# A two-layer attention encoder: the latent heads' keys and queries read from their banks at full height and put in place by transfers, weight sums two groups later

## The chip, the cores and the metric

One core of a Trainium2 chip runs the whole program in one launch. The metric is the device time of an execution in microseconds (us).

## What is computed

Two encoder layers on x of 1024 tokens by 1024 features, in float32; cut to what matters here:

```python
for layer in range(2):
    shift, scale, gate = split(silu(c) @ ada_w[layer] + ada_b[layer], 3)
    h = rms_norm(x, norm_w[layer]) * (1 + scale) + shift
    y = even_mixer(h) if layer == 0 else odd_mixer(h)
    x = x + gate * y
return rms_norm(x, final_norm)

# even_mixer: group A, dense grouped-query attention (8 heads, 2 of keys), and group B, latent attention:
cq, ckv = rms_norm(cq, g1), rms_norm(ckv, g2)      # 256 and 128 wide
qb = (cq @ w_uq).reshape(b, s, 8, 64 + 32)         # per head: 64 plain and 32 rotary
q_nope, q_rope = qb[..., :64], apply_rope(qb[..., 64:])
scores = (q_nope @ w_uk) @ ckv + q_rope @ k_rope   # 8 heads, one rotary key for all
out = concat([oa * silu(ga), ob * silu(gb)]) @ w_out
# odd_mixer: attention in a window of 128 either way, 16 heads, then (oc * silu(gc)) @ w_out
```

## The kernel before

Every matrix product takes its operands as a high and a low part, and three matmuls (high by high, low by high, high by low) make one product. The instructions are not issued in the order of the code. A recorder (L115 to L570) notes each operation, and `run` (L259) puts them into an order by a list schedule: each operation has a cost (`cost`, L224), a priority from its place, and a tile or PSUM bank to wait for (49 tiles of 128x1024 "u", 8 banks); a transfer's landing is guessed there too. `emit` (L543) issues the result, so every instruction of the profile carries L551. Within an engine the order is fixed from then on; SyncE's queue (SP) is such an engine, so a transfer that has to wait holds those behind it.

Layer 0's attention is 32 groups n = 0 to 31, each one head and one half of the queries: scores, maximum, exponential (tiles Pa in group A, Pb in group B), scaling by the reciprocal sum (POOL), transposes (TensorE), a copy and a difference that make the high and low part (hla, hlb), and the product with the values. n = 0 to 15 are group A, n = 16 to 31 group B, two groups to a head and four to a pair of heads. In a tile's name Pb201 is head 2, half 0, query block 1.

`before(n)` (L1467) hangs preparation on the groups:

- `b_heads(p, half)` (L1397) makes the keys and queries of heads 2p and 2p+1 for one half, at n = 15 (pair 0, both halves), 19 (pair 1), 22 and 23 (pair 2), 27 (pair 3); they are used from n = 16, 20, 24 and 28. A bank kn or qn of 128x512 holds two heads, 64 rows each. The tiles k1, k2, q1, q2 need the high and low part of a head on particular 64 rows, in part crossed over: q1 and k1 carry the high part on rows 0 to 63 and rotary rows above; k2 and q2 hold high and low parts one above the other. Every part is made by an operation of its own, 64 rows high: per call 6 copies on ACT, 4 differences on DVE, 2 copies on POOL.
- The rotary rows of the queries (qrh, qrl: high and low part, by ACT and DVE) go to memory as qr_sp by SP, and come back into q1[64:128] by four transfers of 128 KB a pair on POOL's queue.
- `weight_sums` (L1458), at n = 17 to 24 by the table `WS_AT`, makes the sums of blocks of the output weights for later: a load of 512 KB into a tile ws (SP), then up to three times an accumulating transfer from w_out (POOL's queue, `accum_op`) and a store of the sum so far (SP). Each link waits for the landing of the last; each tile of ws stays taken till its last store.

```python
1463        for a, b, k in [(3, 1, 0)] if third else [(1, 1, 1), (2, 0, 0), (4, 0, 1)]:
1464            nc.gpsimd.dma_start(out=t, in_=w(b, k), accum_op=ALU.add)
1465            nc.sync.dma_start(out=ws_sp[l, a, j], in_=t)
```

`wino_out` (L1569) is the output projection of each layer, in a form with fewer products that uses these sums. `layer1_after` (L1515) follows the second one: the statistic of the final norm for each half (`rstd_rows`, L742), and `finish`, which scales and stores. The last `finish` takes 256 tokens, of which the rows sit in four tiles xr110 to xr113. Layer 1's windowed attention writes its outputs by 64x128 blocks (`win_PV`, L1887) into tiles og1, multiplies them by the gates (`g_ft`, `g_ft_late`), and spills those that have to wait for the projection. At the start, TensorE does `WARM` transposes that nothing reads, 20 of them between the first statistic and the first product of layer 0.

Of the kernel before, what the change touches and what calls it, by code (L numbers as in the profile page):

```python
# [14 lines left out]
ALU = mybir.AluOpType  # L15
# [4 lines left out]
P = 128  # L20
# [34 lines left out]
WARM = (32, 14, 20)  # L55
# [4 lines left out]
WS_AT = {17: ((0, 0, False),), 18: ((0, 0, True),), 19: ((0, 1, False),), 20: ((0, 1, True),),  # L60
         21: ((1, 0, False),), 22: ((1, 0, True),), 23: ((1, 1, False),), 24: ((1, 1, True),)}
# [53 lines left out]
class Recorder:  # L115
# [143 lines left out]
    def run(self):  # L259
# [131 lines left out]
        while started < N or ev:  # L391

            for e in engs:
# [5 lines left out]
                while h:  # L399
# [12 lines left out]
                    if e == "SP" or (o.call[0].__name__ == "dma_start"):  # L412
                        nb = 4 * max(self._region(v)[2] * max(1, self._region(v)[3])
                                     for v in list(o.call[1]) + list(o.call[2].values())
                                     if isinstance(v, VP) or hasattr(v, "tensor"))
                        dma_free = max(dma_free, t + 1300) + nb / (205.0 if "accum_op" in o.call[2] else 410.0)
                        fin = dma_free + 500
                        busy[e] = t + (450 if e == "SP" else o.dur)
                    else:
                        fin = o.end  # L420
                        busy[e] = o.end
# [152 lines left out]
def encoder_kernel(ctx: ExitStack, tc: tile.TileContext, xt, ada_t, w_c1, w_c2, w_c3, w_g0, w_uq, w_ukv, w_out0, w_v1,  # L574
# [74 lines left out]

    def rstd_of(ss, n, width):  # L650
        v = SM("v")
        nc.gpsimd.tensor_scalar(v[:, :width], ss, 1.0 / n, EPS, op0=ALU.mult, op1=ALU.add)
        r = SM("r")
        nc.gpsimd.tensor_tensor(out=r[:, :width], in0=v[:, :width], in1=mhalf[:, :width], op=ALU.pow)
        return r
# [86 lines left out]
    def rstd_rows(accs, name):  # L742
# [21 lines left out]
        pr = PA(f"rb{name}")  # L764
        for j in range(nt):
            m_ = nc.tensor.transpose(out=pr[:, j * P:(j + 1) * P], in_=r[:, j:j + 1].broadcast_to([P, P]), identity=ident)
        if name == "x0" and WARM[2]:
            warm(WARM[2], m_)
        return pr[:, 0:n]
# [149 lines left out]
    for kc in range(KC):  # L919
# [3 lines left out]
        if kc == 0:  # L923
            rb0 = rows_copy(rp0, "x0")
# [3 lines left out]
        modulate(0, kc, chunk(xT[0], kc), None, hT0[0][kc], "normed")  # L928
        for i in range(E1):
            c1_part(i, w1[kc:], [kc])  # L930
# [466 lines left out]
    def b_heads(p, half):  # L1397
        e, o = 2 * p, 2 * p + 1
        for h in (e, o) if half == 0 else ():
            q1[h], q2[h], k2[h] = UR(f"q1{h}"), UR(f"q2{h}"), UR(f"k2{h}")  # L1400
            nc.gpsimd.dma_start(out=q1[h][64:96, :], in_=qr_sp[0][h * 32:(h + 1) * 32, :])
            nc.gpsimd.dma_start(out=q1[h][96:128, :], in_=qr_sp[1][h * 32:(h + 1) * 32, :])
# [6 lines left out]
        nc.scalar.copy(k1[0][0:64, c], ps[0:64, :])  # L1409
        nc.scalar.copy(k2[o][64:128, c], ps[64:128, :])  # L1410
        nc.scalar.copy(k1[1][0:64, c], ps[64:128, :])
        K2E(k2[e][0:64, c], f(k1[0][0:64, c]))
        sub(k2[e][64:128, c], ps[0:64, :], f(k1[0][0:64, c]))
        sub(k2[o][0:64, c], ps[64:128, :], f(k2[o][64:128, c]))
# [5 lines left out]
        nc.scalar.copy(q1[e][0:64, c], ps[0:64, :])  # L1420
        nc.scalar.copy(q1[o][0:64, c], ps[64:128, :])
        nc.scalar.copy(q2[e][64:128, c], ps[0:64, :])
        K2E(q2[o][0:64, c], f(q1[o][0:64, c]))
        sub(q2[e][0:64, c], ps[0:64, :], f(q1[e][0:64, c]))
        sub(q2[o][64:128, c], ps[64:128, :], f(q1[o][0:64, c]))
# [89 lines left out]
    def layer1_after():  # L1515
# [4 lines left out]
        def finish(res, half, c0, n, pr, last):  # L1520
            if not last:
                rb = rows_copy(pr, f"z{half}{c0}")

            with rec.at(shift=0 if last or half == 0 else 300):
                for k2 in (0, 1, 2, 3) if half == 0 else (2, 3, 0, 1):
# [4 lines left out]
                    if last or half == 1 and k2 > 1:  # L1530
                        r_ = pr if last else rb
                        (nc.vector if last else nc.gpsimd).tensor_tensor(
# [8 lines left out]
        def after(half, ft, c0, n, pos, res, last):  # L1541
# [17 lines left out]
            if pos == 7:  # L1559
                finish(res, half, c0, n, rstd_rows(sums, f"z{half}{c0}"), last)  # L1560
# [8 lines left out]
    def wino_out(l, w, kept, at, res_src, after):  # L1569
# [5 lines left out]
        def raw_o(half, k2, mark):  # L1575
            gone = [e for e in range(2) if 2 * k2 + e not in kept]
# [241 lines left out]
    def g_ft(p):  # L1818
        def evac(half, ps):
            sl = og1[p][:, half * 512:(half + 1) * 512]  # L1820
# [4 lines left out]
            if half == 1 and p < 6:  # L1825
                spill_out(1, p, og1.pop(p))
# [4 lines left out]
    def g_ft_late(p):  # L1831
        def evac(half, ps):
            if half == 0:
                g1[p] = U(f"g1{p}")
            sl = g1[p][:, half * 512:(half + 1) * 512]
            nc.scalar.activation(sl, ps, AF.Tanh, scale=0.5)
            nc.vector.scalar_tensor_tensor(out=sl, in0=sl, scalar=1.0, in1=ps, op0=ALU.add, op1=ALU.mult)
# [49 lines left out]
    def win_PV(g, i, Ps, lo, n, og):  # L1887
# [16 lines left out]
        for j in range(4):  # L1904
            r = slice((j % 2) * 64, (j % 2) * 64 + 64)
            nc.vector.tensor_tensor(out=og[j // 2][r, i * P:(i + 1) * P], in0=acc[0:64, j * P:(j + 1) * P],
                                    in1=tmp[:, j * P:(j + 1) * P], op=ALU.add)
# [32 lines left out]
    for g in range(4):  # L1940
        win_bias(g)
        for j in range(2):
            og1[2 * g + j] = U(f"og1{g}{j}")
        for i in range(NT):
# [3 lines left out]
            if True:  # L1948
                cur = (g, i) + win_S(g, i) + ([og1[2 * g], og1[2 * g + 1]],)
# [9 lines left out]
    for j in (6, 7):  # L1959
        nc.gpsimd.tensor_tensor(out=og1[j], in0=og1[j], in1=g1[j], op=ALU.mult)  # L1960
        keep[j] = og1[j]
# [81 lines left out]
```

## Time and profile before

| | us |
|---|---|
| median of three runs | 1184.37 (1184.14 to 1184.73) |
| the profiled execution | 1186.49 |
| its span, first to last instruction | 1184.7 |
| TensorE busy in the span | 1144.0 (97%) |
| VectorE / ScalarE / GpSimd busy | 961.6 (81%) / 699.6 (59%) / 608.0 (51%) |
| mean granted TensorE clock | 0.991 |

The span is 1.8 us short of the execution's time. A matmul row counts as busy from its start to its modelled end, so neighbouring rows overlap; what TensorE lost is read from the time in which it had nothing (rows 2 of the section below) and from stretches in which the granted clock is under 1.00.

### The profile page before, as it was taken

To read this page: it belongs to the slowest core of one execution; us is meant where nothing else is said; L and a number is where in the kernel's file an instruction comes from. 1 tells how busy PE (TensorE), PEld (TensorE's weight loads), DVE (VectorE), ACT (ScalarE), POOL (GpSimd) and SP (SyncE) were. 2 spreads that over 40 slices of the span, in tenths; PEclk is the share of its full clock that TensorE was granted. 3 is DMA by queue.
4 is the path that set the end of the run, shared out by engine and by line. 5 is a ranking of instruction groups with operands and counts; after the bars stand their busy time and mean duration, and the time that the engine had idled before them with its cause. 6 is when DMAs were issued, how large, how long until landed. Compare 5 with 4: busy or idle time off the path is not lost.

```text
span 1184.7 us, 17555 instructions
## 1 busy us (share of the span) xinstructions
PE 1144.0 (97%) x6080; PEld 961.5 (81%) x6080; DVE 961.6 (81%) x1743; ACT 699.6 (59%) x1405; POOL 608.0 (51%) x592
## 2 busy tenths in 40 slices
PE   8999999999999999799999999999999999999996
PEld 7898877878878778588878787988888888888885
DVE  8974889888887987678889988968887488776986
ACT  5553356566655777677678842336765366565723
POOL 1344496857855566354436352714465265445424
PEclk9999999999999999999999999999999999999999
DMA  9602423232122189671116343400111122046413
GB/s 370 249 1 72 168 104 124 90 125 93 64 63 82 74 214 247 163 198 38 36 72 240 116 142 113 171 18 2 37 45 63 54 73 72 19 160 228 127 38 142
DMA packets 42441, 133.44 MB, mean 113 GB/s; under 512 B 4592, under 2 KB 9200, under 8 KB 42352
## 3 DMA queue, kind: packets, MB, share of 16 engines
q1 hardware_dynamic: 38192, 120.78, 28.6%
q0 software_dynamic: 3072, 10.49, 4.9%
q8 instruction: 48, 0.79, 0.3%
q10 hardware_dynamic: 1088, 1.05, 0.3%
q14 instruction: 41, 0.34, 0.1%
HBM read 101.24 MB, written 31.06 MB: 112 GB/s over the span
## 4 chain that ended last, share of the span: by engine, by line
PE 78%; DVE 10%; ACT 4%; DMA 3%; issue 2%; POOL 2%; SPq 0%; POOLq 0%; DVEq 0%; ACTq 0%
PE psum L551 78%; DVE nm L551 2%; DMA ws<-in_w_out 2%; DVE p L551 1%; DVE hla L551 1%; DMA ws<-ws 1%; DVE xr L551 1%; ACT Pa L551 1%; DMA xT<-in_xt 1%; ACT q L551 1%; DVE t40l L551 0%; POOL r L551 0%; POOL sq L551 0%; DVE hl L551 0%; ACT p L551 0%
## 5 line engine op out<-in xcount | busy, mean ns | idle before, releaser
L551 DVE TENSOR_REDUCE nm<-psum 128x1 f32<-128x1024 f32 x128 | 154.6, 1216 | 26.4 <-PE psum L551 24.8
L551 POOL TENSOR_SCALAR p<-p,dn 128x384 f32<-128x384 f32 (+1 forms) x128 | 72.5, 587 | 163.1 <-DVE dn L551 85.4
L551 PE MATMUL psum<-hla,VA 128*128 128x512 f32 x256 | 94.4, 428 | 7.9 <-DVE hla L551 5.4
L551 POOL TENSOR_SCALAR Pa<-Pa,rs 128x1024 f32<-128x1024 f32 x64 | 79.0, 1242 | 40.2 <-DVE rs L551 37.5
L551 ACT ACTIVATE Pb<-psum,nm 128x1024 f32<-128x1024 f32 x64 | 71.9, 1125 | 36.0 <-DVE nm L551 30.3
L551 ACT CAST hla<-psum 128x512 fp32r<-128x512 f32 x128 | 71.4, 597 | 37.0 <-PE psum L551 31.2
L551 DVE TENSOR_TENSOR hla<-psum,hla 128x512 fp32r<-128x512 f32 x128 | 83.7, 681 | 11.4 <-ACT hla L551 10.9
L551 PE MATMUL psum<-hlb,VB 128*128 128x512 f32 x256 | 90.6, 426 | 2.2 <-DVE hlb L551 1.5
L551 ACT ACTIVATE Pa<-psum,nm 128x1024 f32<-128x1024 f32 x64 | 71.7, 1122 | 33.6 <-DVE nm L551 28.4
L551 PE MATMUL psum<-ident,Pa 128*128 128x128 f32 x512 | 89.2, 273 | 0.8 <-DVE q L551 0.6
L551 POOL TENSOR_SCALAR Pb<-Pb,rs 128x1024 f32<-128x1024 f32 x64 | 73.3, 1195 | 30.5 <-DVE rs L551 27.6
L551 DVE TENSOR_TENSOR hlb<-psum,hlb 128x512 fp32r<-128x512 f32 x128 | 82.1, 683 | 7.6 <-ACT hlb L551 6.7
L551 PE MATMUL psum<-k,q 128*128 128x512 f32 x256 | 86.2, 408 | 1.0 <-ACT Pb L551 1.0
L551 PE MATMUL psum<-ident,Pb 128*128 128x128 f32 x512 | 79.7, 273 | 7.3 <-POOL Pb L551 6.7
L551 DVE CUSTOM_DVE_ANT_0 p<-psum,bias,rows_g 128x384 f32<-128x384 f32 (+1 forms) x128 | 70.5, 578 | 12.2 <-PE psum L551 10.9
L551 PEld LDWEIGHTS psum<-ident,Pb 128*128 128x128 f32 x512 | 63.2, 140 | 19.4 <-POOL Pb L551 7.3
L551 ACT ACTIVATE p<-p,nm 128x384 f32<-128x384 f32 (+1 forms) x128 | 74.1, 585 | 7.7 <-DVE nm L551 7.7
L551 ACT COPY ot<-psum 64x512 f32<-64x512 f32 x64 | 37.4, 584 | 65.2 <-PE psum L551 64.5
L551 ACT CAST hlb<-psum 128x512 fp32r<-128x512 f32 x128 | 69.2, 604 | 10.2 <-PE psum L551 7.8
L551 PEld LDWEIGHTS psum<-ident,Pa 128*128 128x128 f32 x512 | 64.2, 141 | 11.9 <-DVE q L551 0.8
L551 PEld LDWEIGHTS psum<-hla,VA 128*128 128x128 f32 x256 | 46.7, 191 | 20.6 <-DVE hla L551 9.4
L551 ACT CAST hl<-psum 128x512 fp32r<-128x512 f32 x88 | 46.6, 593 | 27.9 <-PE psum L551 22.0
(891 smaller groups left out, 3671.1 us busy)
## 6 DMA issues: line engine op xcount, KB each, us to landing
ada<-in_ada_t SPq DMA_DIRECT2D x32, 512.0 KB, 7.1
adag<-in_ada_t SPq DMA_DIRECT2D x16, 512.0 KB, 4.9
ws<-in_w_out POOLq DMA_DIRECT2D x16, 512.0 KB, 6.2
ws<-ws SPq DMA_DIRECT2D x16, 512.0 KB, 3.1
S<-ws SPq DMA_DIRECT2D x16, 512.0 KB, 4.4
o<-spill SPq DMA_DIRECT2D x12, 512.0 KB, 5.8
A<-in_w_out SPq DMA_DIRECT2D x12, 512.0 KB, 5.8
xT<-in_xt SPq DMA_DIRECT2D x8, 512.0 KB, 8.1
```

Source lines behind the costliest of these rows:

```text
L551: fn(*[real(v) for v in a], **{k: real(v) for k, v in kw.items()})
```

## The change

- In `b_heads`, `two_parts` reads a bank once as a whole: the high part of both heads by one 128x512 copy on ACT, the low part by one 128x512 difference on DVE, into a tile. Six transfers of 64x512 (128 KB) on SP's queue (`put`) then bring the parts to k1, k2, q1, q2. Twelve a call, 96 in all, take the place of 48 ACT copies less 16, 32 DVE differences less 16, and 16 POOL copies.
- The 16 transfers of rotary rows move from POOL's queue to SP's.
- `WS_AT` is two groups later for each entry, and the planner counts 3000 ns instead of 500 to the landing of an accumulating transfer.
- The third number of `WARM` is 8, not 20; ACT's copy of the first statistic's rows comes after the first modulation.
- The last `finish` has the rows of 1/rms in two banks; one is copied to a tile, by which POOL scales xr112 (before: DVE).
- Layer 1's og1 tiles are laid out by half of the tokens, with two blocks of 512 columns each, so that `win_PV` needs two DVE operations instead of four, and the spills, the late gates and the last products follow that layout.

```diff
-WARM = (32, 14, 20)
+WARM = (32, 14, 8)
-WS_AT = {17: ((0, 0, False),), 18: ((0, 0, True),), 19: ((0, 1, False),), 20: ((0, 1, True),),
-         21: ((1, 0, False),), 22: ((1, 0, True),), 23: ((1, 1, False),), 24: ((1, 1, True),)}
+WS_AT = {19: ((0, 0, False),), 20: ((0, 0, True),), 21: ((0, 1, False),), 22: ((0, 1, True),),
+         23: ((1, 0, False),), 24: ((1, 0, True),), 25: ((1, 1, False),), 26: ((1, 1, True),)}
-                        fin = dma_free + 500
+                        fin = dma_free + (3000 if "accum_op" in o.call[2] else 500)
+    def two_parts(ps, name, scale=None):
+        t = UR(name)
+        h, l = t[:, 0:512], t[:, 512:1024]
+        if scale is None:
+            nc.scalar.copy(h, ps)
+            sub(l, ps, f(h))
...
+        return [[x[e * 64:(e + 1) * 64, :] for x in (h, l)] for e in range(2)]
+    def put(o, i):
+        nc.sync.dma_start(out=f(o), in_=f(i))
-            nc.gpsimd.dma_start(out=q1[h][64:96, :], in_=qr_sp[0][h * 32:(h + 1) * 32, :])
+            nc.sync.dma_start(out=f(q1[h])[64:96, :], in_=qr_sp[0][h * 32:(h + 1) * 32, :])
...
-        nc.scalar.copy(k1[0][0:64, c], ps[0:64, :])
-        nc.scalar.copy(k2[o][64:128, c], ps[64:128, :])
-        nc.scalar.copy(k1[1][0:64, c], ps[64:128, :])
-        K2E(k2[e][0:64, c], f(k1[0][0:64, c]))
-        sub(k2[e][64:128, c], ps[0:64, :], f(k1[0][0:64, c]))
-        sub(k2[o][0:64, c], ps[64:128, :], f(k2[o][64:128, c]))
+        (he, le), (ho, lo) = two_parts(ps, f"knp{p}{half}")
+        for d, r, x in ((k1[0], 0, he), (k2[e], 0, he), (k2[e], 64, le), (k1[1], 0, ho), (k2[o], 64, ho), (k2[o], 0, lo)):
+            put(d[r:r + 64, c], x)
...
-        def finish(res, half, c0, n, pr, last):
-            if not last:
+            if last:
+                pr, p2 = pr
+                rb = rows_copy(p2, f"z{half}{c0}")
+            else:
                 rb = rows_copy(pr, f"z{half}{c0}")
...
-                        r_ = pr if last else rb
-                        (nc.vector if last else nc.gpsimd).tensor_tensor(
+                        dve = last and k2 != 2
+                        r_ = pr if dve else rb
+                        (nc.vector if dve else nc.gpsimd).tensor_tensor(
...
-        for j in range(4):
-            r = slice((j % 2) * 64, (j % 2) * 64 + 64)
-            nc.vector.tensor_tensor(out=og[j // 2][r, i * P:(i + 1) * P], in0=acc[0:64, j * P:(j + 1) * P],
-                                    in1=tmp[:, j * P:(j + 1) * P], op=ALU.add)
+        for e in range(2):
+            nc.vector.tensor_tensor(out=o[e * 64:(e + 1) * 64, :, (i % 4) * P:(i % 4 + 1) * P],
+                                    in0=by(acc[0:64, :])[:, :, e, :], in1=by(tmp)[:, :, e, :], op=ALU.add)
```

How the order moves, at three places. On POOL, around the scalings of head 2's first group (n = 20), before; ws100, ws101 and ws110 are weight sums of layer 1, q23 and k22 parts of pair 1:

```order
L551 TENSOR_SCALAR k22_880<-k12_678 64x512
L551 DMA ws100_936<-in_w_out1 128x1024
L551 TENSOR_SCALAR q23_882<-q13_881 64x512
...
L551 DMA ws100_936<-in_w_out1 128x1024
L551 TENSOR_TENSOR og('0', 4)_849<-og('0', 4)_849,gB0_798 64x512
L551 DMA ws101_963<-in_w_out1 128x1024
L551 TENSOR_SCALAR Pb200_920<-Pb200_920,rs_922 128x1024
L551 TENSOR_SCALAR Pb201_924<-Pb201_924,rs_926 128x1024
```

and of the change:

```order
L551 DMA ws000_879<-in_w_out0 128x1024
L551 DMA ws010_942<-in_w_out0 128x1024
L551 TENSOR_TENSOR og('0', 4)_852<-og('0', 4)_852,gB0_802 64x512
...
L551 TENSOR_TENSOR og('0', 4)_852<-og('0', 4)_852,gB0_802 64x512
L551 TENSOR_SCALAR Pb200_926<-Pb200_926,rs_928 128x1024
L551 DMA ws010_942<-in_w_out0 128x1024
L551 DMA ws011_969<-in_w_out0 128x1024
L551 TENSOR_SCALAR Pb201_930<-Pb201_930,rs_932 128x1024
```

Before, three links of chains stand in a row ahead of Pb200; now one scaling is ahead of the next two links, and the chains there are those of layer 0.

On SP, the puts of pair 1 and what stands around them in the change (knp and qnp are the new tiles; a row with ws on both sides of the arrow is a store of a sum to memory, one with in_w_out a load):

```order
L551 DMA ws020_254<-ws000_879 128x1024
L551 DMA ws010_942<-in_w_out0 128x1024
L551 DMA ws030_256<-ws001_915 128x1024
...
L551 DMA k12_678<-knp10_886 64x512
L551 DMA ws040_258<-ws000_879 128x1024
L551 DMA k22_882<-knp10_886 64x512 x2
L551 DMA k10_676<-knp10_886 64x512
...
L551 DMA q12_880<-qnp10_887 64x512
```

All of pair 1's puts but one stand behind the store of the third sum of ws000; before, no key or query passed through this queue.

On POOL at the end, before:

```order
L551 TENSOR_TENSOR r_1848<-ss_1847,mhalf_78 128x2
L551 TENSOR_TENSOR sq21_1829<-sq21_1829,sq212561_1851 128x256
L551 TENSOR_TENSOR xr112_1746<-xr112_1746,rbz10_1849 128x512
L551 TENSOR_TENSOR sq21_1829<-sq21_1829,sq212562_1852 128x256
L551 TENSOR_TENSOR xr113_1747<-xr113_1747,rbz10_1849 128x512
L551 TENSOR_TENSOR r_1856<-ss_1855,mhalf_78 128x2
```

and of the change:

```order
L551 TENSOR_TENSOR r_1864<-ss_1863,mhalf_78 128x2
L551 TENSOR_TENSOR r_1872<-ss_1871,mhalf_78 128x2
L551 TENSOR_TENSOR xr112_1762<-xr112_1762,rbz10_1865 128x512
L551 TENSOR_TENSOR xr113_1763<-xr113_1763,rbz10_1865 128x512
L551 TENSOR_TENSOR xr112_1762<-xr112_1762,rbz1256_1873 128x512
```

The two scalings by the first statistic (rbz10) stood ahead of the second one's r; now they and a third scaling come behind it.

## Rows read from the trace of the kernel before

**Rows 1.** The page's part 1: each engine's busy us, its share of the span, and its instructions.

```profile
PE 1144.0 (97%) x6080; PEld 961.5 (81%) x6080; DVE 961.6 (81%) x1743; ACT 699.6 (59%) x1405; POOL 608.0 (51%) x592
```

**Rows 2.** The table of stretches of the span: the stretch, its length, then busy time of PE, PEld, DVE, ACT and POOL (with the number of instructions), the granted TensorE clock (1.00 is 2.4 GHz, 0.50 is 1.2 GHz), the DMA engines' busy share and what they moved.

```profile
396.00:480.00 84.00, 79.25 (x435) 64.05 (x433) 70.78 (x117) 62.59 (x118) 52.37 (x61) 1.00 0.76 201
480.00:512.00 32.00, 25.36 (x113) 19.43 (x114) 21.25 (x32) 17.09 (x32) 13.51 (x14) 0.89 0.67 171
512.00:660.00 148.00, 144.84 (x797) 118.31 (x795) 130.12 (x202) 116.92 (x215) 73.89 (x68) 1.00 0.32 104
660.00:810.00 150.00, 148.57 (x781) 127.51 (x780) 120.60 (x175) 63.04 (x100) 57.90 (x32) 1.00 0.32 111
810.00:1160.00 350.00, 348.42 (x1768) 293.78 (x1767) 277.70 (x694) 208.62 (x500) 170.45 (x195) 1.00 0.23 78
```

**Rows 3.** The waits of TensorE between 396 and 660 us: what it waited for, us in total, times, longest.

```profile
PE psum L551 <- POOL Pb L551: 6.7, 2, 5.9
PE psum L551 <- DVE hla L551: 3.2, 4, 1.3
...
PE psum L551 <- DVE q L551: 1.0, 3, 0.6
```

**Rows 4.** The timeline of TensorE at the longest of these waits: start, duration, engine, operation, and in brackets the idle time before it and what ended it.

```profile
501.19 0.47 PE L551 MATMUL psum<-ident,Pb 128*128 128x128 f32 x1 [5.92 <-POOL Pb L551]
```

**Rows 5.** The timeline of POOL up to the same moment.

```profile
499.06 0.88 POOL L551 DMA_DIRECT2D ws<-in_w_out  x1 [9.21 <-DMA ws<-in_w_out]
500.02 4.40 POOL L551 TENSOR_SCALAR Pb<-Pb,rs 128x1024 f32<-128x1024 f32 x4
```

**Rows 6.** The timeline of SyncE's queue there: a row's second number is the time from its first issue to the end of its last, its waits included.

```profile
471.19 22.26 SPq L551 DMA_DIRECT2D ws<-ws  x4
493.56 1.21 SPq L551 DMA_DIRECT2D ws<-in_w_out  x2
```

**Rows 7.** Three short stretches, columns as in rows 2: after the long wait, after a wait of 1.83 us for ACT Pa that ended at 171.29, and after the one of 1.32 us that ended at 418.86.

```profile
501.20:507.40 6.20, 6.20 (x16) 4.90 (x17) 2.48 (x3) 1.21 (x2) 5.05 (x5) 0.52 0.75 174
172.00:176.00 4.00, 3.84 (x13) 2.73 (x11) 2.20 (x6) 1.91 (x5) 4.00 (x4) 0.58 0.00 0
420.00:424.00 4.00, 3.42 (x18) 2.33 (x19) 3.66 (x7) 2.19 (x4) 2.49 (x5) 1.00 0.95 171
```

**Rows 8.** The groups of instructions between 396 and 660 us, shapes kept apart: count, busy us and mean ns of one, idle time before. The keys' parts and the rotary rows; the queries' parts are as many.

```profile
L551 ACT CAST k<-psum 64x512 fp32r<-64x512 f32 x24 | 14.0, 582 | 2.3 <-PE psum L551 2.0
...
L551 DVE TENSOR_TENSOR k<-psum,k 64x512 fp32r<-64x512 f32 x16 | 11.0, 688 | 5.0 <-ACT k L551 4.7
...
L551 POOL DMA_DIRECT2D q<-qr_sp x16 | 8.8, 611 | 0.0
```

**Rows 9.** The page's part 5: two groups over the whole span that read a whole bank, 128 partitions high.

```profile
L551 ACT CAST hla<-psum 128x512 fp32r<-128x512 f32 x128 | 71.4, 597 | 37.0 <-PE psum L551 31.2
L551 DVE TENSOR_TENSOR hla<-psum,hla 128x512 fp32r<-128x512 f32 x128 | 83.7, 681 | 11.4 <-ACT hla L551 10.9
```

**Rows 10.** The table of DMA issues: queue, count, KB of one, median us from issue to landing.

```profile
ws<-in_w_out POOLq DMA_DIRECT2D x16, 512.0 KB, 6.2
...
q<-qr_sp POOLq DMA_DIRECT2D x16, 128.0 KB, 4.6
...
qr_sp<-qrl SPq DMA_DIRECT2D x2, 512.0 KB, 4.6
...
kr_sp<-krraw SPq DMA_DIRECT2D x1, 128.0 KB, 1.7
ropeb<-kr_sp SPq DMA_DIRECT2D x1, 128.0 KB, 2.7
```

**Rows 11.** The waits of SyncE's queue from 425 to 515 us.

```profile
SPq L551 <- DMA ws<-in_w_out: 75.6, 13, 10.7
```

**Rows 12.** The timeline of TensorE up to the first scores of group B (k, q), and under it DVE's low parts of the rotary rows.

```profile
418.86 0.73 PE L551 MATMUL psum<-hla,VA 128*128 128x512 f32 x2 [1.32 <-DVE hla L551]
...
423.09 0.55 PE L551 MATMUL psum<-ident,Pa 128*128 128x128 f32 x3 [0.58 <-DVE q L551]
423.60 0.50 PE L551 MATMUL psum<-k,q 128*128 128x512 f32 x1
...
409.49 1.29 DVE L551 TENSOR_TENSOR qrl<-psum,qrh 128x512 fp32r<-128x512 f32 x2
```

**Rows 13.** The timeline of TensorE at the start: the 20 transposes that nothing reads; the first product follows them.

```profile
15.59 4.01 PE L551 MATMUL psum<-ident 128*128 128x128 f32 x20
```

**Rows 14.** The start, the timeline of ACT some 22 us later.

```profile
42.46 1.05 ACT L551 CAST w2h<-w2s 128x1024 fp32r<-128x1024 f32 x1 [0.23 <-DMA w2s<-in_w_c]
43.41 0.81 ACT L551 ACTIVATE hT00h<-xT,mods 128x512 fp32r<-128x512 f32 x1
```

**Rows 15.** Groups of instructions on DVE, shapes kept apart: between 810 and 1160 us the blocks of the windowed attention's outputs, and after 1100 us the scalings of the last layer's first half.

```profile
L551 DVE TENSOR_TENSOR og<-psum,ot 64x128 f32<-64x128 f32 x128 | 36.2, 283 | 18.9 <-ACT ot L551 17.3
...
L551 DVE SCALAR_TENSOR_TENSOR xr<-xr,cols,rbz 128x512 f32<-128x512 f32 x8 | 6.2, 809 | 0.0
```

**Rows 16.** The end, the timelines of POOL (first two rows) and DVE (last).

```profile
1174.58 1.27 POOL L551 TENSOR_TENSOR xr<-xr,rbz 128x512 f32<-128x512 f32 x1
1176.96 0.71 POOL L551 TENSOR_TENSOR r<-ss,mhalf 128x2 f32<-128x2 f32 x1 [1.11 <-DVE ss L551]
...
1178.19 2.48 DVE L551 TENSOR_TENSOR xr<-xr,psum 128x512 f32<-128x512 f32 x4 [1.31 <-PE psum L551]
```

## What was predicted before the change was run

> **What bounds the kernel now.** I read the page's busy times first: TensorE is busy for 1144.0 of 1184.7 us [rows 1], so work taken off VectorE, ScalarE or GpSimd gains nothing by itself. What can be won is the 40.7 us in which TensorE has nothing to do, and the time it runs at its lower clock. The table of stretches says where that is [rows 2]. From 396 to 660 us, the end of group A and group B, TensorE idles 4.75 + 6.64 + 3.16 = 14.55 us (length less busy time of the first three rows). From 660 to 1160 us, nearly all of the output projection and layer 1, it idles only 1.43 + 1.58 = 3.0 us. So the large edits act on group B, and layer 1's can win 3 us at most.
>
> The waits of TensorE name what ends the idle time in group B [rows 3]: POOL's scaling Pb 6.7 us, of which 5.9 in one wait, then hla and q on DVE. The reader should follow the one wait back through three timelines. TensorE waits 5.92 us for a scaled Pb at 501.19 [rows 4]. POOL starts on the Pb tiles at 500.02, but before that it has stood 9.21 us for the landing of an accumulating transfer, to issue the next one at 499.06 [rows 5]. That transfer's chain is late because SP needs 22.26 us for four stores of sums, with the next loads behind them at 493.56 [rows 6]. So the bound here is no engine's work: a link of a chain holds back POOL's scalings in an in-order stream.
>
> The wait costs more than itself. In the 6.2 us behind it TensorE is busy throughout at a mean granted clock of 0.52, mostly its 1.2 GHz level: 6.2 x 0.48 = 3.0 us of work lost. A wait of 1.83 us had a like stretch behind it (0.58), one of 1.32 us did not (1.00) [rows 7]. I count 14.55 + 3.0 = 17.55 us as lost in group B.
>
> **The change, part by part.**
>
> *Sums two groups later.* The order puts each link of a chain behind more scalings: Pb200 then stands before the next link of layer 0's chains rather than behind three links. A link waits for 6.2 us of landing [rows 10], and a group lasts about 14.8 us (423.60, the first score [rows 12], to 660, over 16 groups), in which the new order keeps about one or two links. I take the long wait as gone, with its clock: -5.92 - 3.0 = -8.9 us. Late next would be another scaling behind a link, in the groups 19 to 26; that is the second rival.
>
> *Banks read at full height.* Over the eight calls 48 copies of 64x512 on ACT leave at 0.582 us, 32 differences on DVE at 0.688 us, and 16 copies on POOL [rows 8]. A whole bank takes as long as half of it: 0.597 us and 0.681 us [rows 9]. So 16 + 16 such operations stay. ACT is relieved of 48 x 0.582 - 16 x 0.597 = 18.4 us, DVE of 32 x 0.688 - 16 x 0.681 = 11.1 us. On the path lies only what TensorE waited for: hla 3.2 and q 1.0 us [rows 3], crowded at pair 0's preparation (1.32 and 0.58 us, 1.90 together [rows 12], with 0.8 for hla soon after) and, less so, at pair 3's (0.9 us). I take these 3.6 us as gone and all smaller waits, 14.55 - 5.92 - 3.6 = 5.0 us, as kept.
>
> *Puts and rotary rows on SP.* New is a chain: copy 0.6, difference 0.7, issue, landing. An issue takes SP 1.21/2 = 0.6 us [rows 6], so the 24 puts and 4 rotary rows of a pair fill up to 17 us of its queue. Their landing is bounded by the 128 KB rows [rows 10]: 1.7 us between quiet queues, 2.7 us, and 4.6 us for the rotary rows. I take 2.7 for puts, and 4.6 where the weight sums run beside them. POOL loses 16 issues of 0.611 us [rows 8], which nothing waited for: 0.
>
> Pair 0: the second low rotary part ends at 409.49 + 1.29 = 410.8 us [rows 12], its store is issued by 411.4 and landed 4.6 us later, at 416.0. The load behind it takes 0.6 and 2.7 to 4.6 us: 419.3 to 421.2. Without its two waits of 1.90 us TensorE would be at the scores at 421.7, and with some ten rows fewer ahead of them in the new order at about 420.5. That is a wait of 0 to 0.7 us if SP is free; but the puts of the first half stand between on SP, and two or three of them more make it 1.3. I take 1.3, with ends of 0 and 3.
>
> Pair 1 is prepared at n = 19, one group of 14.8 us ahead, and all but one of its puts stand behind a store that waits for the third accumulation of ws000. SP's waits on these accumulations sum to 75.6 us from 425 to 515, the longest 10.7 [rows 11]. From a bank being ready it takes 0.6 + 0.7 + up to 12 x 0.6 + 4.6 = 13 us to the last put of a half, which fills the group; what SP then waits comes on top. The third link should have landed by then; I take 2.0 us, with ends of 0 and 10.7. Pair 2 has a further group of slack: 0. Pair 3 at n = 27 has the queue to itself but is also one group ahead: 0.6 us, ends 0 and 2.
>
> Group B's losses after: 5.0 + 1.3 + 2.0 + 0.6 = 8.9 us, against 17.55: **-8.6 us**.
>
> *Warm-ups.* Twelve transposes fewer are 12 x 4.01/20 = 2.4 us [rows 13]. But the start runs on transfers: some 22 us on, ACT still waits 0.23 us for a weight's landing before the cast that stands ahead of hT00h, which is done only at 44.2 [rows 14]. TensorE needs that tile at once, so it would idle there or earlier. Taken 0; ends -0.3, and +1.7 if the gathered wait of 2 us costs the clock as the one of 1.83 did (4 x 0.42 = 1.7 [rows 7]).
>
> *Layer 1.* The 128 small operations of `win_PV` at 0.283 us [rows 15] become 64 twice as wide, at between 0.283 and 0.566 us: up to 18 us less on DVE, in a stretch with 1.58 us of idle time [rows 2]. 0, ends -1 and +1. In the projection after it, the order now puts the eight scalings of the first half (0.809 us each, 6.5 us [rows 15]) in one row ahead of an update that the next products wait for: +0.8, ends 0 and 2.
>
> *The end.* POOL did its two scalings before the last r, the second from 1174.58, and r from 1176.96 to 1177.67; DVE finished in 2.48 us from 1178.19, at 1180.67 [rows 16]. Now both and a third follow r: 3 x 1.27 = 3.8 us from about 1177.7, so 1181.5, while DVE has only one operation less. +0.8 us from that, and 0.7 for r's own place behind the other r (0.71): +1.5, ends 0 and 2.5.
>
> **Sum.** -8.6 + 0 + 0 + 0.8 + 1.5 = -6.3 us. The profiled execution took 1186.49 us, its span 1184.7; the median of the runs, 1184.37, is 2.1 us under it. 1186.49 - 6.3 = 1180.2, and by the same distance the median becomes **1178.1 us**.
>
> **A rule against the rows.** A 128 KB transfer took 1.7 to 4.6 us, more where queues were full [rows 10]. The Trainium skill (DMA: Bandwidth & Descriptors, "Anatomy of one DMA") gives about 2.0 us fixed plus bytes over 436 GB/s, which is 2.3 us for a put, wherever it stands. By it the waits of pairs 0, 1 and 3 would vanish and the time be 1178.1 - 3.9 = 1174.2; I stay with the rows.
>
> **Rivals.**
>
> *The puts come late (slower).* SP's in-order queue holds pair 1's puts, and perhaps pair 2's, behind stores that wait for accumulations, as it held loads for 22.26 us [rows 6]. If a hold of 10.7 us [rows 11] meets a pair with some 4 us of slack, TensorE waits 6.7 us, and 3.0 more at the low clock: 9.7. Pairs 1 and 2 both: 1178.1 - 2.0 + 19.4 = 1195.5; one of them: 1185.8. It turns the sign when puts cost TensorE 6.3 + 2.0 = 8.3 us, a wait of 5.3 with its clock. For it: the store that stands ahead in the order. Against it: with the links further apart the store's own link is issued a group earlier. The Trainium skill (the same page and section) says that engines of the DMA don't wait on semaphores, the issuing sequencer does, before dispatch; the trace agrees (22.26 us for four stores [rows 6]), and it is the rule by which this rival works. Chance 0.18, a third of it for one pair only.
>
> *The chain's wait only moves (no change).* POOL still holds scalings behind a link in groups 19 to 26, a wait of some 5.9 us with 3.0 of clock comes back: 1178.1 + 8.9 = 1187.0, or, if a wait is half as long and keeps the clock, 1181. For it: several links in a row are still in POOL's order ahead of Pb201. Against it: two scalings' worth of slack. Chance 0.12, mostly near 1183 to 1186.
>
> *More than forecast.* No put is waited for, small waits on DVE shrink by half with its 11 us less work, and the end is free: 1178.1 - 3.9 - 2.5 - 1.5 = 1170.2. Chance 0.15.
>
> **How the numbers follow.** The forecast has 0.55, with ends of 1173.5 (no put is late: -3.9, and -0.7) and 1183 (+1.7 at the start, +1.7 at pair 0, +1.5 in the layers and at the end). A measurement of this kernel can tell 0.2%, 2.4 us, from no change. Faster by more than that is under 1182.0: nearly all of the forecast, the larger gain, and little of the second rival, 0.70. Slower is over 1186.8: most of the first rival and some of the second, 0.16. Between, 0.14. The range leaves out the far ends of the first rival and of the larger gain: 1170 to 1187.
>
> **What would show it.** In the changed profile, right: no wait for POOL Pb over 2 us from 480 to 560, the clock at 1.00 there, idle time from 396 to 660 near 9 us, waits before k, q matmuls of 1 to 2 us at heads 0, 2 and 6 that end with a transfer; TensorE starting 2.4 us earlier and waiting as long before 45 us; the last transfer leaving some 1.5 us later behind the last matmul than before. Wrong: k, q matmuls that wait 5 us or more for a put, with SP's queue waiting for ws; a long wait for Pb; a gain in layer 1 of over 3 us, or a start that keeps its 2.4 us.

## The result: slower, and the profile after

The change took 1190.32 us in the median of six runs (1187.86 to 1193.01), the kernel before 1184.55 (1182.71 to 1187.59): a ratio of 1.0049, with a 95% interval of 1.0032 to 1.0066. The forecast was 1178.1. The profiled execution is the fastest of the six, 1187.86 us with a span of 1186.1.

The engines were relieved as planned, TensorE was not; the page's busy times after, to hold against [rows 1]:

```profile
PE 1140.8 (96%) x6070; PEld 958.4 (81%) x6070; DVE 933.7 (79%) x1662; ACT 680.2 (57%) x1374; POOL 591.8 (50%) x563
```

For a like comparison I cut both spans at the same events: the start of layer 0's products, its second statistic, a wait in group A that both have, the statistic of layer 1, the last product, the end. The table of stretches (columns as in [rows 2]) of the kernel before:

```profile
10.00:68.36 58.36, 55.43 (x307) 50.75 (x307) 54.80 (x78) 33.36 (x68) 15.54 (x10) 0.97 0.67 264
68.36:345.02 276.66, 269.36 (x1445) 224.95 (x1445) 225.15 (x347) 152.62 (x296) 180.54 (x163) 0.99 0.29 97
345.02:729.49 384.47, 368.49 (x1951) 301.04 (x1951) 323.15 (x480) 262.93 (x467) 198.51 (x186) 0.99 0.43 128
729.49:1173.78 444.29, 442.53 (x2332) 378.01 (x2333) 348.56 (x820) 243.34 (x564) 209.55 (x223) 1.00 0.24 84
1173.78:1184.70 10.92, 1.59 (x9) 0.67 (x7) 5.08 (x12) 1.29 (x3) 2.77 (x4) 0.76 0.56 192
```

and of the change:

```profile
10.00:68.39 58.39, 53.59 (x296) 47.66 (x296) 54.84 (x78) 33.23 (x67) 15.54 (x10) 1.00 0.67 264
68.39:341.16 272.77, 265.83 (x1445) 222.81 (x1445) 224.09 (x347) 152.59 (x296) 181.43 (x163) 1.00 0.29 98
341.16:728.37 387.21, 369.02 (x1950) 302.42 (x1951) 309.97 (x464) 243.58 (x435) 181.18 (x154) 0.98 0.57 159
728.37:1172.92 444.55, 442.31 (x2329) 377.12 (x2329) 334.34 (x752) 242.63 (x563) 206.77 (x223) 1.00 0.24 84
1172.92:1186.10 13.18, 2.30 (x15) 1.26 (x13) 5.61 (x14) 2.03 (x5) 5.82 (x6) 0.71 0.47 160
```

Read length and PE busy time line by line. The start is the same (58.36, 58.39). In the second line the same 1445 matmuls take 3.9 us less in this execution, 3.5 of it in busy time (265.83 against 269.36 us): the clock never fell there, while in the profile before it fell after two waits of 1.83 and 1.95 us. Such stretches come and go between executions: in E1 below, where TensorE has the order of the kernel before, this line is 272.54 us long. So the profiled execution flatters the change by about 3.9 us: the profiles are 1.4 us apart, the medians 5.8. Group B with the projection up to layer 1 (third line) is 2.7 us longer, 387.21 against 384.47, instead of 8.6 shorter. Layer 1 is the same (444.55, 444.29), and the end after the last product is 2.3 us longer (13.18, 10.92).

TensorE's waits in the third stretch, to hold against [rows 3]:

```profile
PE psum L551 <- ACT hlb L551: 4.4, 3, 3.7
PE psum L551 <- DMA q<-qr_sp: 3.3, 1, 3.3
PE psum L551 <- DMA k<-knp: 2.4, 4, 1.3
PE psum L551 <- ACT Pb L551: 2.2, 3, 1.0
PE psum L551 <- DVE hlb L551: 1.9, 3, 0.9
...
PE psum L551 <- POOL Pb L551: 0.6, 1, 0.6
...
PE psum L551 <- DVE hla L551: 0.3, 2, 0.2
```

The long wait for POOL Pb and the waits for hla and q are gone, as forecast. In their place stand one wait of 3.32 us for pair 0's rotary rows, small ones for puts, and one of 3.69 us that names ACT hlb. TensorE's rows of the two long ones, from two stretches of its timeline:

```profile
418.93 1.19 PE L551 MATMUL psum<-k,q 128*128 128x512 f32 x2 [3.32 <-DMA q<-qr_sp]
```

```profile
558.89 0.80 PE L551 MATMUL psum<-hlb,VB 128*128 128x512 f32 x1 [3.69 <-ACT hlb L551]
```

The second must be followed further: ACT itself stood 3.82 us, for the landing of a store of sums,

```profile
558.25 1.56 ACT L551 CAST hlb<-psum 128x512 fp32r<-128x512 f32 x3 [3.82 <-DMA ws<-ws]
```

and that store left SyncE's queue at 553.47, once the accumulation before it had landed:

```profile
553.47 0.34 SPq L551 DMA_DIRECT2D ws<-ws  x1
```

No score waits here for a put. ACT waits for a tile that a weight sum still holds. Behind each of the two long waits the clock stood at half speed for 6.8 us:

```profile
418.00:424.80 6.80, 5.87 (x16) 4.48 (x17) 1.70 (x3) 0.99 (x2) 1.12 (x1) 0.56 0.95 212
557.90:564.70 6.80, 5.81 (x15) 4.63 (x16) 2.60 (x4) 2.15 (x4) 2.24 (x3) 0.55 0.54 145
```

The table of DMA issues after, to hold against [rows 10]:

```profile
ws<-in_w_out POOLq DMA_DIRECT2D x16, 512.0 KB, 6.7
ws<-ws SPq DMA_DIRECT2D x16, 512.0 KB, 4.4
...
k<-knp SPq DMA_DIRECT2D x48, 128.0 KB, 3.1
q<-qnp SPq DMA_DIRECT2D x48, 128.0 KB, 3.3
...
q<-qr_sp SPq DMA_DIRECT2D x16, 128.0 KB, 3.9
```

A put lands in 3.1 to 3.3 us, between the forecast's 2.7 and the 4.6 that it took beside the sums. But what was there already got slower: stores of sums take 4.4 us (3.1 on the page of before), accumulations 6.7 (6.2 in [rows 10]).

### The profile page after: what moved, and what is told of

It reads as the page before. It is cut to its first block, busy times and chain, and to the rows that moved or that the text cites. A ratio compares the mean times of both kernels' runs of the same rounds, so it can differ in the third digit from the quotient of the medians.

```text
span 1186.1 us, 17634 instructions
## 1 busy us (share of the span) xinstructions
PE 1140.8 (96%) x6070; PEld 958.4 (81%) x6070; DVE 933.7 (79%) x1662; ACT 680.2 (57%) x1374; POOL 591.8 (50%) x563
## 4 chain that ended last, share of the span: by engine, by line
PE 75%; DVE 10%; DMA 7%; ACT 3%; issue 2%; SPq 2%; POOL 1%; POOLq 0%; ACTq 0%; DVEq 0%
PE psum L551 75%; DVE nm L551 2%; SPq L551 2%; DMA ada<-in_ada_t 2%; DMA ws<-in_w_out 2%; DVE p L551 1%; DMA ws<-ws 1%; DMA w2s<-in_w_c 1%; DMA w31s<-in_w_c 1%; DMA q<-qnp 1%; DVE xr L551 1%; DVE hl L551 1%; ACT Pa L551 1%; DMA k<-knp 1%; DVE t40l L551 0%
## 5 line engine op out<-in xcount | busy, mean ns | idle before, releaser
L551 DVE TENSOR_TENSOR hl<-psum,hl 128x512 fp32r<-128x512 f32 x88 | 55.6, 683 | 10.8 <-ACT hl L551 10.2
```

Source lines behind the costliest of these rows:

```text
L551: fn(*[real(v) for v in a], **{k: real(v) for k, v in kw.items()})
```

## The experiments

Theories before the first runs: **P**, the transfers of the parts lose the time and the later sums gain it as forecast; **S**, the sums lose it at their new place.

**E1, the later sums alone**, on the kernel before.

```diff
-WS_AT = {17: ((0, 0, False),), 18: ((0, 0, True),), 19: ((0, 1, False),), 20: ((0, 1, True),),
+WS_AT = {19: ((0, 0, False),), 20: ((0, 0, True),), 21: ((0, 1, False),), 22: ((0, 1, True),),
...
-                        fin = dma_free + 500
+                        fin = dma_free + (3000 if "accum_op" in o.call[2] else 500)
```

> The kernel before with the weight sums two groups later and 3000 ns counted for an accumulation's landing; nothing else of the change. Theory P (the transfers of the parts lose the time, the later sums gain it as forecast): no wait for POOL Pb over 2 us, 1175 to 1180 us against 1184.5 of before. Theory S (the sums themselves lose it at their new place, because their tiles are given back late and ACT waits for a tile, as it did for 3.8 us at 558 us of the changed kernel): 1184 to 1189 us, with a wait of ACT hlb or Pb for a store of sums of over 2 us.

1175.04 us, ratio to before 0.9927 (0.9914 to 0.9941): P holds. The third stretch, and one of 80 us among the sums:

```profile
340.77:715.31 374.54, 364.65 (x1950) 298.98 (x1951) 323.47 (x480) 263.22 (x467) 198.67 (x186) 1.00 0.44 131
480.00:560.00 80.00, 79.25 (x439) 65.76 (x438) 69.84 (x113) 60.70 (x113) 46.66 (x47) 1.00 0.77 197
```

TensorE idles 9.9 us in 374.54; the clock does not fall, and the DMA engines are 0.77 busy (last but one number).

**E2, the puts alone**: new `b_heads` with puts and rotary rows on SyncE's queue, sums at their old place.

> The kernel before with the keys' and queries' parts read at full height, put in place on SyncE's queue, and the rotary rows on that queue; sums where they were. Theory P: the wait for pair 0's rotary rows (3.3 us in the changed kernel) with 3.4 us at the lower clock stays, and the stores and loads of sums meet the puts in one queue: 1188 to 1196 us. Theory S: 1180 to 1185 us.

1190.23 us, 1.0057 (1.0042 to 1.0072): P again. Without the later sums too the long wait for POOL Pb went (1.3 us are left, in three), and 11.2 us of waits for k and q took its place.

**E3, the changed kernel with the old last finish.**

```diff
-            if last:
-                pr, p2 = pr
-                rb = rows_copy(p2, f"z{half}{c0}")
-            else:
+            if not last:
                 rb = rows_copy(pr, f"z{half}{c0}")
...
```

> The changed kernel with the last finish as before (one bank of 1/rms, two scalings on POOL by the first statistic, the rest on DVE). Both theories: the last matmul to the end of the span goes from 13.2 back to about 10.9 us, so 2.3 us under the changed kernel: about 1188 us. If the end is no part of the loss: 1190 us.

1192.15 us, 1.0068 (1.0050 to 1.0086). A miss: the stretch behind the last product stays long, so the finish is not what made it longer.

```profile
1177.96:1191.50 13.54, 2.06 (x13) 1.04 (x11) 6.19 (x15) 1.65 (x4) 4.59 (x5) 0.70 0.46 156
```

**E4, the changed kernel with the old heads and the old finish** (later sums, layer 1's layout and the short warm-up are left of the change).

> The changed kernel with the parts made by ACT, DVE and POOL as before, the rotary rows on POOL's queue, and the last finish as before; the later sums, layer 1's layout and the shorter warm-up stay. Theory P: 1175 to 1180 us. Theory S: 1184 to 1189 us. If both are half true, 1181 to 1184 us.

1177.76 us, 0.9952 (0.9937 to 0.9966). The third stretch takes 374.63 us, as in E1, so the puts cost 387.21 - 374.63 = 12.6 us of the changed kernel, after what they save on ACT and DVE (E4 still waits 4.6 us for hla and q, the changed kernel 0.3); and the end is long without the new finish (second row).

```profile
345.89:720.52 374.63, 364.86 (x1950) 299.14 (x1951) 322.73 (x480) 263.10 (x467) 198.59 (x186) 1.00 0.44 131
1165.22:1178.10 12.88, 2.24 (x13) 1.04 (x11) 6.02 (x15) 1.65 (x4) 4.56 (x5) 0.69 0.48 163
```

Next, where in the puts: **R**, the rotary rows on SyncE's queue; **L**, keys that come through memory queues are late by their chain; **Q**, tiles and queues shared with the sums.

**E5, rotary rows back on POOL's queue.**

```diff
-            nc.sync.dma_start(out=f(q1[h])[64:96, :], in_=qr_sp[0][h * 32:(h + 1) * 32, :])
+            nc.gpsimd.dma_start(out=q1[h][64:96, :], in_=qr_sp[0][h * 32:(h + 1) * 32, :])
```

> The changed kernel (1190.3 us) with the 16 transfers of rotary rows back on POOL's queue; the puts stay on SyncE's. Theory R (the rotary rows in SyncE's queue are the loss, 3.3 us of wait for pair 0 with 3.4 us at half clock behind it): no wait for q from qr_sp over 1 us, 1183 to 1186 us. Theory L (keys and queries that come through memory queues are late by their chain, whichever row is last): another row is waited for in its place, 1188 to 1191 us.

1192.06 us, 1.0072 (1.0050 to 1.0094): R falls, and L's range is missed by 1.1 us. Pair 0's wait became two of 0.8 us for k, and the wait for the tile stayed within 0.01 us:

```profile
564.67 0.80 PE L551 MATMUL psum<-hlb,VB 128*128 128x512 f32 x1 [3.68 <-ACT hlb L551]
```

**E6, everything one group earlier** (`B_AT` 13 for the rotary rows, 18, 21 and 22, 26 for pairs 1 to 3).

> The changed kernel with the preparation of the latent heads one group earlier: rotary rows at n = 13, pair 1 at 18, pair 2 at 21 and 22, pair 3 at 26. Theory L: the waits for puts (2.4 us), for rotary rows (3.3 us) and one of the two stretches at the lower clock go, 1181 to 1185 us. Theory Q (the loss is in tiles and in queues shared with the sums, not in the head start): 1187 to 1192 us, with waits of ACT for stores of sums as before.

1196.07 us, 1.0108 (1.0084 to 1.0133). It says nothing on head start: at n = 21 pair 2 overwrites keys that head 2's second half still uses, so the computation is another one. E10 is the sound form.

**E7, no accumulations.**

```diff
-            nc.gpsimd.dma_start(out=t, in_=w(b, k), accum_op=ALU.add)
```

> The changed kernel without the accumulating transfers: each sum's tile is loaded and stored three times as it is, so the output projection works with other weights. Theory Q: the wait of ACT hlb for a tile (3.7 us at 559 us, with 3.4 us at half clock) goes, and the puts of pair 1 are no longer behind a store that waits: 1181 to 1185 us. Theory L: only the one wait for a tile goes, the waits for rows of pairs 0, 1 and 3 stay: 1185 to 1188 us.

1178.57 us, 0.9961 (0.9946 to 0.9977), 2.4 us better than Q's range, and away from L's. The third stretch is as long as that of a kernel without puts (374.63 in E4), with the DMA engines at 0.57,

```profile
344.46:719.32 374.86, 363.31 (x1950) 299.94 (x1951) 309.70 (x464) 243.42 (x435) 166.91 (x138) 1.00 0.45 142
480.00:560.00 80.00, 78.98 (x436) 65.69 (x437) 65.52 (x107) 54.79 (x104) 31.37 (x28) 1.00 0.57 173
```

and a put lands in 2.4 us:

```profile
k<-knp SPq DMA_DIRECT2D x48, 128.0 KB, 2.4
q<-qnp SPq DMA_DIRECT2D x48, 128.0 KB, 2.4
```

Pair 0's wait for its rotary rows stays (2.78 us). So the loss needs both, the puts and the accumulations. This run takes away the accumulations' bytes and the waits for them together; E9, E11 and E13 go into that.

**E8, later sums and layer 1's layout**, old finish, long warm-up.

> The kernel before with the later sums and layer 1's layout by halves, the warm-up of 20 and the old end; the later sums alone measured 1175.0 us. If the layout is what moves the end (last product to the end of the span 12.9 us and not 10.9, as with the old finish in the changed kernel): 1177 us, and the last two transposes of r come 9.7 us ahead of the end, not 7.0. If the shorter warm-up made the 2.7 us between 1175.0 and 1177.8 us: 1175 us.

1176.41 us, 0.9939 (0.9920 to 0.9958); the end takes 12.95 us:

```profile
1163.85:1176.80 12.95, 2.24 (x13) 1.05 (x11) 6.03 (x15) 1.66 (x4) 4.56 (x5) 0.69 0.47 162
```

The longer end comes with the layout: it makes the order put the first block's statistic behind the last product, whichever finish is used. POOL's first r starts 1.4 us after the last product here (1165.27), and started 2.8 us ahead of it in the kernel before (1170.95).

For what puts and sums share: **O**, SyncE's order, puts behind stores that wait; **D**, the capacity of the DMA engines.

**E9, stores that wait for no accumulation.**

```diff
-            nc.sync.dma_start(out=ws_sp[l, a, j], in_=t)
+            nc.sync.dma_start(out=ws_sp[l, a, j], in_=f(B["krl"]))
```

> The changed kernel with the 16 stores of sums taken from another tile that no accumulation writes, so that SyncE's queue no longer waits for an accumulation; the accumulations and all transfers stay, and the projections work with other weights. Theory O (order: puts stand in SyncE's queue behind stores that wait): 1177 to 1183 us, like the kernel without accumulations (1178.6). Theory D (the DMA engines themselves are full between 480 and 560 us, 0.93 to 0.97 busy, so every landing is late): 1186 to 1192 us with the busy share unchanged.

1193.75 us, 1.0076 (1.0057 to 1.0095): O, as stated, falls, as far as a kernel can show it whose order was planned anew; D's range is missed by 1.8 us, and the share from 480 to 560 us is 0.88, not unchanged. SyncE's queue no longer waits for an accumulation, and TensorE waits as long. The stores now leave without that wait and take 6.3 us to land (4.4 in the changed kernel), so a put can still stand behind them.

```profile
PE psum L551 <- ACT Pb L551: 5.5, 2, 4.5
PE psum L551 <- DMA k<-knp: 5.3, 4, 3.0
PE psum L551 <- DMA q<-qr_sp: 3.4, 1, 3.4
```

**E10, pairs 1 and 3 and the rotary rows one group earlier.**

> The changed kernel with pairs 1 and 3 and the rotary rows prepared one group earlier (n = 18, 26, 13), pair 2 where it was, so that no key is overwritten before its last use. If head start is what is missing: the 3.3 us before pair 0 and 2.4 us of waits for puts go with a stretch at the lower clock, 1181 to 1186 us. Theory D: pair 1 only meets other sums, 1187 to 1193 us.

1191.45 us, 1.0053 (1.0035 to 1.0071). Head start removes waits for k and q (1.2 us are left) but POOL Pb waits again, 6.2 us in six.

**E11, puts that nothing reads**, added to E1.

```diff
+        for nm, src in (("dk", k1[0]), ("dq", q1[e])):
+            t = UR(f"{nm}{p}{half}")
+            for x in range(6):
+                r, w_ = x // 2 % 2 * 64, x % 2 * 512
+                nc.sync.dma_start(out=f(t)[r:r + 64, w_:w_ + 512], in_=f(src)[0:64, c])
```

> The kernel before with the later sums (1175.0 us), parts made by the engines as before, and 96 further transfers of 64x512 on SyncE's queue from finished keys and queries into tiles that nothing reads. No score waits for them. Theory D: the busy share of the DMA engines from 480 to 560 us rises from 0.77 to over 0.9, landings of sums get later, tiles come back late: 1180 to 1187 us. Theory O, and any theory in which only the scores' own dependence on puts costs: 1174 to 1178 us.

1185.24 us, 0.9999 (0.9987 to 1.0010): all of E1's gain is gone, although no score waits for these transfers. They differ from the real puts in one thing: of each six the last two write where the first two did, so SyncE's queue waits for a landing there (in E13 too).

```profile
342.97:728.35 385.38, 367.98 (x1951) 302.29 (x1951) 321.44 (x480) 262.02 (x467) 200.44 (x186) 0.99 0.57 160
480.00:560.00 80.00, 71.02 (x365) 57.79 (x364) 58.47 (x94) 50.78 (x96) 39.67 (x41) 0.94 0.86 209
```

The old wait is back, within 0.04 us of [rows 4]:

```profile
496.39 0.48 PE L551 MATMUL psum<-ident,Pb 128*128 128x128 f32 x1 [5.96 <-POOL Pb L551]
```

since POOL stands for the landing of a store of a sum before it may issue the next accumulation, with the Pb tiles behind it:

```profile
492.68 0.91 POOL L551 DMA_DIRECT2D ws<-in_w_out  x1 [8.69 <-DMA ws<-ws]
...
495.21 4.42 POOL L551 TENSOR_SCALAR Pb<-Pb,rs 128x1024 f32<-128x1024 f32 x4
```

**E12, sums spread out** to n = 17, 18, 20, 21, 24, 25, 28, 29 in the changed kernel.

> The changed kernel with the sums spread out to n = 17, 18, 20, 21 for layer 0 and 24, 25, 28, 29 for layer 1, so that they lie less upon one another and upon the puts of pairs 1 and 2. Theory D: busy share from 480 to 560 us at 0.8 or less, 1181 to 1187 us. Theory O: a store waits ahead of pair 1's puts as before, 1187 to 1193 us.

1190.84 us, 1.0050 (1.0033 to 1.0066). A miss for D as I had put it, and in O's range: the share from 480 to 560 us fell to 0.69, but pair 3, which had waited under 1 us in all, now waits 4.2 us, with a store of sums among its puts on SyncE's queue (596.65):

```profile
607.96 1.22 PE L551 MATMUL psum<-k,q 128*128 128x512 f32 x2 [2.90 <-DMA k<-knp]
```

**E13, the idle puts cut to one row each.** The order on TensorE, ACT and DVE is that of E11, instruction by instruction. On POOL and in SyncE's queue the planner, which counts a transfer's bytes, moved a few rows.

```diff
-                nc.sync.dma_start(out=f(t)[r:r + 64, w_:w_ + 512], in_=f(src)[0:64, c])
+                nc.sync.dma_start(out=f(t)[r:r + 1, w_:w_ + 512], in_=f(src)[0:1, c])
```

> The kernel with the later sums and 96 transfers that nothing reads (1185.2 us), each cut from 64 rows of 512 to one row of 512; the order of the instructions on TensorE stays. If the bytes in the DMA engines are what the sums meet: busy share from 480 to 560 us back near 0.77, no wait for POOL Pb over 2 us, 1175 to 1178 us. If it is the 96 issues on SyncE's queue: 1182 to 1187 us as with the whole transfers, the wait for POOL Pb of 6 us stays.

1174.44 us, 0.9917 (0.9894 to 0.9939).

```profile
343.69:717.67 373.98, 363.72 (x1951) 299.44 (x1951) 321.42 (x480) 261.76 (x467) 199.77 (x186) 1.00 0.44 132
480.00:560.00 80.00, 78.00 (x424) 64.10 (x423) 68.08 (x110) 58.23 (x109) 43.78 (x45) 1.00 0.69 182
```

96 issues cost nothing; the 63 further rows of each cost about 10 us (0.9999 against 0.9917). Where they do can be read from TensorE, which has one order in both. In its profile E11 falls 7.2 us behind E13 at the long wait and 4.3 us more from 540 to 560 us. Ahead of the long wait only puts, rotary rows and one scaling of group A changed places. There POOL waits for the same store of a sum to land before it issues the next accumulation. From the store's issue that takes 6.65 us in E11,

```profile
474.39 0.54 SPq L551 DMA_DIRECT2D ws<-ws  x1
481.04 0.91 POOL L551 DMA_DIRECT2D ws<-in_w_out  x1 [5.79 <-DMA ws<-ws]
```

and 3.58 us in E13:

```profile
472.95 0.53 SPq L551 DMA_DIRECT2D ws<-ws  x1
476.53 0.91 POOL L551 DMA_DIRECT2D ws<-in_w_out  x1 [1.42 <-DMA ws<-ws]
```

The other 4.3 us lie behind places where the chain of ws100 stands earlier in E13's order, so they are not shown to be the rows' alone. The Trainium skill (DMA: Bandwidth & Descriptors, "Issuing engines are not separate DMA queues") says that spreading transfers over issuing engines saves only sequencer time. E5, which moved 16 of the 112 transfers that the change puts on SyncE's queue, agrees as far as it goes: it gained nothing. No run here issues the puts themselves from another engine.

**E14 and E15, sums in group A**, with the rest of the change and without it (`WS_AT` at n = 2 to 10).

> The changed kernel with the sums at n = 2 to 10, in group A, so that no accumulation runs beside the puts; everything is computed. If the meeting of puts and sums is the loss: 1176 to 1181 us, near the kernel without accumulations (1178.6). If group A has no room for them in tiles or queues, the waits come back there: 1184 us or more.

> The kernel before with the sums at n = 2 to 10 and nothing else of the change but the 3000 ns. If the sums cost nothing in group A: 1173 to 1177 us, as with the sums two groups later (1175.0). If group A has no room: 1180 us or more.

1193.51 us, 1.0074 (1.0053 to 1.0095), and 1190.61 us, 1.0054 (1.0034 to 1.0073). Group A has no room: there TensorE waits up to 5.2 us for hla, so neither is a way out. But group B and the projection (from one event that both have, to layer 1's statistic) tell what was asked. With puts,

```profile
354.48:730.72 376.24, 364.73 (x1955) 300.65 (x1956) 311.77 (x467) 244.74 (x438) 169.09 (x138) 1.00 0.35 108
```

and without:

```profile
358.29:733.82 375.53, 365.76 (x1956) 300.01 (x1956) 324.68 (x483) 264.42 (x470) 186.58 (x170) 1.00 0.21 75
```

With the sums elsewhere the puts cost 376.24 - 375.53 = 0.7 us, not 12.6.

## Why the prediction was wrong

**The later sums** were right: forecast -8.9 us, measured alone -0.73% of 1184.55, 8.6 us, with the third stretch 384.47 - 374.54 = 9.9 us shorter in the profiles.

**The relief of ACT and DVE** was right as far as it went: the waits for hla and q, 4.2 us [rows 3], are down to 0.3.

**The step that failed is "Puts and rotary rows on SP"**, priced at 1.3 + 2.0 + 0.6 = 3.9 us. With the 3.6 us of relief set against it, the two together were to cost 0.3 us, and they cost 12.6 (E4). What the step did look at, the waits for the new transfers, was near: 5.7 us, of them 3.3 for pair 0 (just past its end of 3), 1.5 for pair 1 and 0.9 for pair 3. Where no accumulation ran beside them, the puts with their relief did cost 0.7 us (E14, E15). Two things were missing.

First, the step asked only who waits for the new transfers, not what they do to those already there. The sums had the DMA engines 0.77 busy (E1); the puts bring them to 0.95 in the same 80 us of the changed kernel. Then stores and accumulations land late, a sum holds its tile too long, and ACT or POOL, each in order, stands in front of TensorE's next operand: the 3.7 us for hlb. E11, E13 and E7 show it from both sides: idle transfers alone do it, cut to one row each they don't, and without the accumulations the real ones don't.

Second, each such wait cost the clock again. The sum had 3.0 us for the wait that went, and none for a wait that came. The third stretch idles 18.19 us against 9.77 in E4 (387.21 - 369.02 and 374.63 - 364.86), 8.4 more; the two low stretches (0.56 and 0.55 of 6.8 us) take up to 6.0 more, part of it hidden in time in which operands were late anyway. Together up to 14.4, measured 12.6.

The prediction's own signs did not find this. No k, q matmul waited 5 us and no long wait for Pb was left, so none of its signs of being wrong showed; but TensorE idled 16.5 us from 396 to 660 us, not near 9, and the clock from 480 to 560 was 0.98.

**The first rival had the sign, not the place.** It put the loss on scores that wait for puts held up behind accumulations in SyncE's order. Waits do sit on the issuing queue there, but E9 takes them away and nothing comes back. **The rule set against the rows**, the Trainium skill's fixed time plus bytes (DMA: Bandwidth & Descriptors, "Anatomy of one DMA"), is stated there for transfers that GpSimd issues; put to the puts, which SyncE issues, it gave an estimate of 2.3 us. The runs are near it where no accumulation runs, 2.4 us in E7, and not beside them, 3.1 to 3.3; by it the forecast would have been further off.

**Warm-ups**: right, 0 (58.36 and 58.39 us). TensorE began its products at 17.32 and waited in four places for hT00. **Layer 1**: 444.55 against 444.29; the 0.8 us for the scalings was 0.3 at most.

**The end**: forecast +1.5, measured +2.3, but for the wrong reason. The timeline of POOL after shows the three scalings behind r as foreseen:

```profile
1175.65 0.70 POOL L551 TENSOR_TENSOR r<-ss,mhalf 128x2 f32<-128x2 f32 x1 [0.60 <-DVE ss L551]
1176.32 3.72 POOL L551 TENSOR_TENSOR xr<-xr,rbz 128x512 f32<-128x512 f32 x3
```

yet with the old finish, without the third scaling, the end takes 13.54 us (E3) and 12.88 (E4), and with the layout alone 12.95 (E8). What costs is the order that layer 1's layout brings.

What stays open: whether a sum's transfers land late because all the DMA engines are full or because a store stands behind puts in the one queue that SyncE feeds. The stores slowed more (2.9 us in E4, 4.4 in the changed kernel) than the accumulations on POOL's queue (6.1 and 6.7), and no run issues the puts elsewhere. Open too are why the clock falls after a wait of about 1.9 us in one execution and not in another, and how much of E12's and E10's loss is the same meeting of transfers at other places, which I read from their waits only.

## What to carry to other kernels

A transfer that takes work off busy engines isn't free because its own reader has slack: look at how busy the DMA engines are in that stretch, and price what the traffic does to transfers that are already there and to the tiles they hold. Two edits of opposite sign can share a change: the sums alone give 0.9927 (E1) and beat both kernels, and only a run of each edit by itself shows that. And where TensorE is 97% busy, a wait is priced with the half-speed stretch that can follow it, for waits that come as for waits that go.

## What the runs showed of the hardware that was not expected

- The DMA engines were 0.95 busy while they moved only 237 GB/s (changed kernel, 480 to 560 us). In the first of the page's 40 slices of the same execution a like share, 0.9 or more, moved 369 GB/s. So near-full engines came at two thirds of the bytes in group B; without the accumulations it was 173 GB/s for a share of 0.57 (E7).
- 96 issues of one row of 2 KB each on SyncE's queue cost the kernel nothing (E13, 1174.44 us against 1175.04 without them); with 64 such rows each it was 1185.24 us.
- The same 1445 matmuls of group A took 272.8 us (changed kernel) or 276.7 (before), by whether the clock fell after two waits of 1.8 to 2.0 us that are there either way: 3.9 us between two executions, two thirds of the effect measured here.
